# The NSA gate's columns as heads and rests in one stationary of 64 columns, with every queue's order dealt anew

## The chip, the cores and the metric

The kernel runs on one core of one Trainium2 chip. The metric is the device time of one execution in microseconds (us); the kernel before has a median of 608.55 us in three runs.

## The reference, cut to what matters

One layer of a hybrid decoder is computed for a prompt of 512 rows and for 8 sample rows. All 520 rows share one wide input projection, and one small part of it, `a_g`, is the gate of the native sparse attention: 24 columns, three for each of 8 heads.

```
h = x * (1.0 + scale[:, None, :]) + shift[:, None, :]
parts = jnp.split(h @ w_in, np.cumsum(IN_WIDTHS)[:-1], axis=-1)
(a_q, a_kc, a_vc, a_ks, a_vs, a_kw, a_vw, a_g, a_z, b_q, b_k, b_v, b_z, m_a, m_b) = parts
...
o_a = nsa_attention(a_q..., jax.nn.sigmoid(a_g.reshape(bsz, t, NSA_KV, NSA_REP, 3)), ...)
...
return gc[..., 0:1] * o_c + gc[..., 1:2] * o_s + gc[..., 2:3] * o_w
```

The rest: compressed-block, selected-block and sliding-window attention, a second attention over blocks (MoBA), SiLU gates, two up-projections, a merge, an output projection and a layer norm. The sample rows read their keys and values from paged caches in device memory.

## The kernel before

**Products in two parts.** The projection runs on TensorE in fp32r with each fp32 operand split into a head (the value rounded to fp32r) and a rest (value less head). A product is three: head by head, rest of the weights by head of the input, head of the weights by rest of the input. The input, modulated and turned, lies in `hTh` (heads) and `hTl` (rests), 8 blocks of 128 channels by 520 rows. The 520 rows are taken in two halves of 260 (`HB`, `HALF`), one PSUM bank each, so one 128-column part of the projection is 8 blocks x 2 halves x 3 products.

**Weights.** `Feed` loads weights (`load_to`), splits them into heads (ScalarE, L445) and rests (VectorE or GpSimd, L446, by way of L367) in tiles `hl` of two rows of 512 columns (`split_to`), and hands them to `dense` (L688), which issues the products. For the gate `dense("ag", 24)` uses 24 columns for each of the 8 blocks: 192 columns of heads, 192 of rests, 48 products with a stationary of 24 columns. `gen_gates` (L767) reads each half's bank with a Tanh on ScalarE (L771); `gates` (L774) turns the result with five transposes on TensorE, makes the sigmoid of it on VectorE (L779, L781) and hands the samples' values on by small DMAs.

**What runs beside the gate.** The gate belongs to the first list of fills (`FILLS[0]`), which is merged with `phis` (L1130): the compression of cached keys and values, whose pages arrive as `craw` and are split by ScalarE (L1007) and by VectorE or GpSimd (L1008, shown as L367) into tiles `u`, and multiplied into the banks `s`.

**Narrow groups.** Attention's products of probabilities with values (`value`, L1240, bank `o`) have stationaries of 64 columns, and the products for the samples (`dec_a`, `dec_b`, bank `e`) and of the modulation (`ada`, `gen_gate`, bank `s`) of 32 columns; these operands are plain fp32. The dense parts, the scores and the up and output projections are fp32r. One set of products outside the gate has an fp32r stationary below 64 columns: `out_samples` (L1693), 16 columns.

**Order.** `line_up` (L329) fixes the order of each engine's instructions: `QUEUES` holds for each engine a list of places in the order in which the program makes them. `SLOTS` holds which of its buffers each tile takes, in turn; `ps.d` are the three PSUM banks of the dense parts. In both kernels the gate's first half has bank 2 of them and its second half bank 0, and the next dense part takes bank 2 and bank 0 after them. An instruction that waits holds back all that stand behind it on its engine; SP issues nearly all DMAs.

Of the kernel before, what the change touches and what calls it, by code (L numbers as in the profile page):

```python
# [11 lines left out]
AF = mybir.ActivationFunctionType  # L12
# [59 lines left out]
for _name, _w in (("ident", 128), ("seli", 10), ("rowmask", 1), ("ones", 1), ("p16", 1),  # L72
# [24 lines left out]
    "ps.d": "01201201201120112102102102102102102102110120120120120120120122201201201201201221021101201201201201201201201210210210210210210210210210210210"
        "21021",
    "ring.whl": "012012012012012012012012012012012012012012012012012012012012012012012012012012012012012012012012201201201201201",
    "phi.craw": "01230130123012301230",  # L100
# [4 lines left out]
    "at.qx": "0120120120120120",  # L105
    "at.mg": "01010101010101",
    "at.sm": "012345670123456701234567012345670123456701234567012345670123456701234567012345670123456701234567",
    "at.p3": "010101010101010101010101",
    "de.cr": "01201201201201201201201202101201201201201201",
# [19 lines left out]
0-1 5-8 2-3 9-12 20-23 4 13-19 24-49 61-63 50-52 56-57 53-55 58-60 67-69 95-97 64-66 92-94 123-125 70-77 86-88 81-83 89-91 84-85 120-122 78-80 98-105  # L129
109-111 106-108 117-119 148-150 114-116 112-113 126-133 151-153 140-141 179-181 137-139 145-147 142-144 134-136 162-164 154-161 176-178 207-209  # L130
168-169 165-167 170-172 182-189 204-206 222-224 196-197 173-175 201-203 198-200 193-195 190-192 210-218 225-227 231-257 228-230 258-275 219-221
276-281 306-311 324-326 312-317 327-329 351-354 330-332 282-287 333-335 288-293 318-323 336-338 406 339-341 294-299 342-344 358-363 345-350 364-366
300-305 367-372 355-357 373-399 407-412 400-405 413-424 431-435 483-485 425-430 486-488 436-441 489-491 448-453 492-494 442-447 495-497 454-459
498-503 507-509 504-506 460-463 510-515 464-469 516-521 482 531-536 522-527 470-475 528-530 537-542 476-481 555-560 543-554 561-566 579-584 567-572
591-596 585-590 597-602 573-578 672-677 603-608 624-635 648-653 636-638 654-656 639-644 657-659 645-647 609-611 660-671 618-623 696-707 678-689
612-617 720-725 690-695 726-731 708-713 765-767 714-719 768-776 789-794 732-737 795-797 777-779 738-743 780-782 744-749 798-800 783-785 750-755
813-818 786-788 801-809 825-830 810-812 819-824 837-842 849-854 831-836 756-764 855-872 843-848 873-884 906-914 966-971 915-923 885-890 924-926
891-896 927-935 942-947 972-977 936-941 948-959 990-995 897-902 960-965 978-983 903-905 984-989 996-1013 1035-1040 1023-1028 1041-1046 1029-1034
1047-1058 1014-1022 1071-1076 1059-1064 1113-1120 1065-1070 1107-1112 1077-1094 1145 1095-1100 1158 1127-1132 1101-1106 1183-1184 1133-1138 1121-1126
1152-1157 1139-1144 1146-1151 1159-1164 1177-1182 1185-1192 1165-1176 1193-1205 1212 1206-1211 1219-1230 1213-1218 1298-1299 1247-1252 1231-1236  # L140
1243-1246 1237-1242 1253-1258 1284-1285 1260-1265 1272-1277 1259 1266-1271 1278-1283 1306-1307 1314-1319 1300-1305 1320-1321 1328-1329 1286-1297
1336-1337 1344-1345 1322-1327 1330-1335 1308-1313 1352-1355 1338-1343 1346-1351 1362-1367 1382-1387 1380-1381 1376-1379 1374-1375 1356-1361 1368-1373
1388-1405 1412-1417 1406-1411 1418-1433 1458-1463 1436-1437 1434-1435 1468-1473 1444-1447 1474-1475 1448-1449 1456-1457 1438-1443 1450-1455 1464-1467
1476-1483 1506-1517 1504-1505 1494-1495 1484-1493 1522-1523 1502-1503 1524-1529 1496-1501 1534-1547 1566-1571 1530-1533 1558-1563 1518-1521 1576-1579
1548-1551 1564-1565 1580-1585 1572-1575 1552-1557 1586-1599 1602-1607 1600-1601 1628-1635 1616-1627 1658-1659 1612-1615 1660-1665 1674-1681 1642-1645
1636-1641 1608-1611 1652-1657 1646-1651 1668-1673 1666-1667 1682-1687 1690-1695 1700-1705 1688-1689 1726-1731 1734-1739 1742-1747 1708-1713 1706-1707
1718-1725 1766-1769 1696-1699 1748-1753 1740-1741 1756-1761 1754-1755 1714-1717 1778-1783 1792-1795 1732-1733 1770-1777 1806-1809 1784-1791 1816-1817
1762-1765 1800-1805 1810-1815 1796-1799 1829-1834 1844-1849 1827-1828 1854-1859 1824-1826 1835-1840 1842-1843 1850-1853 1841 1818-1823 1860-1863
1900-1903 1924-1927 1882-1884 1872-1875 1885-1887 1864-1865 1890-1895 1866-1871 1876-1881 1896-1899 1910-1915 1904-1909 1930-1935 1888-1889 1928-1929
1952-1957 1918-1923 1984-1989 1960-1965 1916-1917 1970-1973 1998-2001 1940-1943 1958-1959 1974-1979 1936-1939 1982-1983 1944-1951 2016-2017 2002-2009  # L150
1966-1969 2018-2023 2010-2015 2032-2037 2067-2072 1980-1981 2075-2080 1990-1997 2044-2049 2054-2059 2038-2043 2028-2031 2065-2066 2024-2027 2061-2064
2089-2092 2060 2099-2100 2050-2053 2081-2088 2073-2074 2101-2106 2111-2112 2153-2154 2107-2110 2093-2098 2119-2124 2129-2130 2137-2140 2131-2136
2113-2118 2125-2128 2155-2158 2165-2168 2141-2146 2169-2174 2185-2186 2147-2152 2175-2180 2187-2192 2213-2218 2197-2198 2219-2224 2181-2184 2209-2212
2193-2196 2199-2204 2159-2164 2231-2236 2227-2228 2205-2208 2225-2226 2271-2272 2255-2256 2229-2230 2241-2254 2257-2260 2237-2240 2267-2270 2303-2306
2273-2282 2291-2294 2283-2284 2297-2302 2261-2266 2307-2308 2295-2296 2309-2314 2285-2290 2335-2336 2319-2324 2315-2316 2337-2342 2317-2318 2349-2354
2343-2346 2325-2328 2355-2364 2329-2334 2347-2348 2365-2368 2375-2376 2411-2422 2369-2374 2409-2410 2423-2424 2435-2438 2377-2408 2439-2440 2471-2482
2441-2442 2483-2486 2443-2444 2461-2462 2425-2428 2455-2460 2429-2434 2487-2488 2463-2468 2513-2514 2451-2454 2489-2500 2469-2470 2445-2450 2515-2526
2501-2512 2531-2536 2561-2566 2537-2542 2545-2550 2527-2530 2551-2556 2575-2580 2557-2560 2543-2544 2583-2588 2567-2572 2635-2640 2633-2634 2573-2574
2581-2582 2621-2632 2647-2652 2641-2646 2589-2616 2682-2683 2617-2620 2750-2757 2684-2687 2758-2765 2688-2693 2663-2664 2653-2658 2665-2674 2659-2662
2694-2699 2675-2680 2700-2705 2736-2737 2681 2724-2735 2706-2707 2720-2723 2708-2719 2768-2779 2738-2749 2766-2767 2780-2785 2839-2840 2804-2807  # L160
2792-2803 2786-2791 2853-2854 2821-2826 2808-2813 2827-2832 2861-2864 2871-2872 2820 2814-2819 2847-2852 2855-2860 2833-2838 2883-2888 2841-2846
2879-2882 2891 2906-2907 2865-2870 2873-2878 2900-2905 2889-2890 2914-2915 2898-2899 2892-2897 2923-2924 2908-2913 2943-2948 2917-2922 2929-2934
2961-2966 2969-2974 2925-2928 2949-2950 2967-2968 2935-2942 2916 2991-2992 2951-2960 2979-2990 2975-2976 3015-3020 2977-2978 3029-3034 2993-2998
3009-3012 3003-3008 3035-3036 2999-3002 3021-3024 3013-3014 3054-3059 3037-3042 3074-3081 3025-3028 3046-3051 3043-3045 3064-3069 3094-3099 3052-3053
3082-3085 3060-3063 3086-3091 3070-3073 3112-3115 3138-3141 3092-3093 3108-3111 3100-3101 3122-3123 3102-3107 3124-3129 3156-3157 3116-3121 3142-3149
3130-3137 3150-3155 3178-3179 3184-3189 3168-3171 3196-3201 3164-3167 3190-3193 3180-3183 3194-3195 3224-3229 3158-3163 3210-3211 3242-3247 3172-3177
3218-3221 3202-3209 3212-3217 3274-3279 3258-3263 3222-3223 3230-3233 3248-3249 3234-3241 3250-3253 3284-3287 3380-3383 3254-3257 3264-3273 3298-3303
3288-3293 3280-3283 3310-3315 3324-3329 3294-3297 3336-3341 3330-3335 3306-3309 3342-3345 3376-3379 3316-3319 3346-3357 3384-3395 3358-3363 3412-3417
# [175 lines left out]
def build(tc, A):  # L344
# [14 lines left out]
    D = {}  # L359
# [12 lines left out]
    with ExitStack() as es:  # L372
# [35 lines left out]
        class Feed:  # L408
# [23 lines left out]
            def split_to(self, u):  # L432
                while self.ns <= u and self.ns < len(self.units):
# [9 lines left out]
                    if len(src.shape) == 3:  # L443
                        h, l = (t.rearrange("p (a b) -> p a b", a=src.shape[1]) for t in (h, l))
# [1534 lines left out]
```

## Time and profile before

| | us |
|---|---|
| median of three runs (lowest to highest) | 608.55 (608.54 to 608.65) |
| the profiled execution: its time | 609.99 |
| the profiled execution: its span | 608.2 |
| the gate's two Tanh, start | 59.23 and 63.33 |
| PE's last product ends near | 600 |

The profile has one line for each engine's busy time (PE is TensorE's products, PEld its weight loads, DVE VectorE, ACT ScalarE, POOL GpSimd, SP the queue that issues DMAs), a chain of the work that ended last, groups of instructions and waits. Nearly all products are recorded under one helper's line, L351, and the splits into rests under L367, so tiles tell them apart: `d<-hTh,hl 128*24` is a product into bank d from the moving tile hTh and the stationary hl of 128 rows and 24 columns. Products are pipelined: the time of one is its passage, and a busy engine may still have gaps shorter than a passage; the distance between two starts shows the pace. In an entry of waits, the numbers are the total in us, how often, and the longest.

### The profile page before, as it was taken

The page shows a single profiled execution, that of the slowest core. Times are in us where ns is not written, and L with a number is a line of the kernel's source. Part 1 is how long each engine was busy: PE and PEld are TensorE (multiplying, and loading weights), DVE is VectorE, ACT ScalarE, POOL GpSimd, SP SyncE. Part 2 cuts the span into 40 slices and gives each one's busy share as a digit, 9 for nine tenths or more (in the row PEclk, how much of TensorE's full clock was granted, in tenths as well). Part 3 has the DMA queues.
Part 4 walks back from the last instruction along what each step waited for, and adds up shares of the span by engine and source line. Part 5 has one row for each costly group of instructions (what it writes and reads, how often), then busy time and mean ns, then how long its engine had stood idle before and what let it go on. Part 6 is the DMA issues. An engine that isn't in the chain of part 4 may idle for free.

```text
span 608.2 us, 13223 instructions
## 1 busy us (share of the span) xinstructions
PE 590.1 (97%) x4737; PEld 501.8 (82%) x4737; DVE 287.8 (47%) x822; ACT 290.5 (48%) x686; POOL 267.5 (44%) x317
## 2 busy tenths in 40 slices
PE   7999999999999999999999999999999999999994
PEld 4789899999997879778768898997777788889774
DVE  1454455423383567445353435686531144435187
ACT  2457456454555546545435363674632342324343
POOL 0202686372445235434318534546441355554306
PEclk9999999999999999999999999999999999999998
DMA  8987166703555676368888661348899886434403
GB/s 283 405 320 254 43 200 176 247 31 98 151 152 160 190 259 213 121 216 286 273 285 284 246 231 30 113 146 287 301 314 338 312 288 241 144 112 142 172 1 140
DMA packets 63955, 124.79 MB, mean 205 GB/s; under 512 B 8402, under 2 KB 26258, under 8 KB 63378
## 3 DMA queue, kind: packets, MB, share of 16 engines
q1 hardware_dynamic: 62482, 119.76, 58.8%
q0 software_dynamic: 1408, 4.20, 2.1%
q8 instruction: 37, 0.61, 0.4%
q14 instruction: 28, 0.23, 0.1%
HBM read 114.34 MB, written 9.58 MB: 204 GB/s over the span
## 4 chain that ended last, share of the span: by engine, by line
PE 78%; DVE 6%; DMA 5%; ACT 4%; POOL 3%; issue 2%; SPq 1%; POOLq 0%; ACTq 0%; DVEq 0%
PE d L351 45%; PE s L351 13%; PE e L351 7%; PE o L351 6%; PE pt L354 4%; PE pt L351 2%; DMA raw<-mobk 1%; DMA z<-xT 1%; ACT u L1007 1%; SPq L357 1%; DMA raw<-w_cols 1%; DMA raw<-w_up 1%; POOL p L1228 1%; DMA craw<-cmp 1%; DVE hl L367 1%
## 5 line engine op out<-in xcount | busy, mean ns | idle before, releaser
L351 PE MATMUL d<-hTh,hl 128*128 128x260 f32 (+1 forms) x1408 | 267.3, 288 | 1.4 <-ACT ev L771 1.2
L351 PEld LDWEIGHTS d<-hTh,hl 128*128 128x128 f32 (+1 forms) x1408 | 216.2, 187 | 6.5 <-issue 1.4
L351 PE MATMUL d<-hTl,hl 128*128 128x260 f32 (+1 forms) x704 | 198.7, 282 | 0.0
L367 POOL TENSOR_TENSOR hl<-raw,hl 128x512 fp32r<-128x512 f32 x57 | 74.4, 1307 | 139.9 <-ACT hl L445 118.5
L351 PEld LDWEIGHTS d<-hTl,hl 128*128 128x128 f32 (+1 forms) x704 | 131.1, 186 | 0.3
L445 ACT CAST hl<-raw 128x512 fp32r<-128x512 f32 x111 | 67.4, 617 | 81.0 <-PE d L351 46.5
L1226 ACT ACTIVATE p<-s,sm 128x512 f32<-128x512 f32 (+3 forms) x96 | 50.6, 528 | 67.8 <-DVE sm L1223 51.3
L1228 POOL TENSOR_SCALAR p<-p,sm,gp 128x512 f32<-128x512 f32 (+3 forms) x64 | 42.0, 666 | 72.7 <-DVE sm L1227 41.8
L367 DVE TENSOR_TENSOR hl<-raw,hl 128x512 fp32r<-128x512 f32 (+1 forms) x54 | 42.1, 783 | 49.8 <-ACT hl L445 44.5
L351 PE MATMUL d<-yh,hl 128*128 128x260 f32 x256 | 47.4, 285 | 0.0
L351 PEld LDWEIGHTS d<-yh,hl 128*128 128x128 f32 x256 | 40.1, 188 | 3.2 <-ACT yh L851 0.8
L354 PE MATMUL pt<-cst,p 128*128 128x128 f32 x240 | 39.4, 278 | 1.2 <-POOL p L1228 0.8
L1223 DVE CUSTOM_DVE_ANT_0 s<-s,band 128x256 f32<-128x256 f32 (+1 forms) x48 | 17.3, 367 | 41.6 <-PE s L351 33.7
L351 PE MATMUL d<-yl,hl 128*128 128x260 f32 x128 | 36.1, 284 | 0.2 <-DVE yl L367 0.2
L354 PEld LDWEIGHTS pt<-cst,p 128*128 128x128 f32 x240 | 27.4, 141 | 9.5 <-issue 3.1
L351 PE MATMUL s<-kd,q 128*128 128x256 f32 (+3 forms) x96 | 33.5, 351 | 1.5 <-DVE c L1269 0.8
L1236 ACT COPY pp<-pt 128x512 f32<-128x512 f32 (+1 forms) x48 | 22.9, 478 | 24.8 <-PE pt L354 23.8
L351 PE MATMUL s<-u,w1h 128*128 128x256 f32 (+1 forms) x160 | 33.5, 281 | 0.1
L351 PE MATMUL o<-pp,v 128*64 128x512 f32 (+3 forms) x192 | 30.7, 444 | 0.0
L351 PE MATMUL s<-kd,qx 128*128 128x256 f32 (+3 forms) x96 | 30.5, 323 | 0.0
L1228 POOL TENSOR_SCALAR p<-p,sm,cst 128x384 f32<-128x384 f32 (+3 forms) x32 | 21.1, 667 | 16.3 <-DVE sm L1227 16.2
L1221 DVE TENSOR_REDUCE sm<-s 128x1 f32<-128x128 f32 (+1 forms) x48 | 16.5, 352 | 24.3 <-PE s L351 20.6
(411 smaller groups left out, 1037.2 us busy)
## 6 DMA issues: line engine op xcount, KB each, us to landing
raw<-w_cols SPq DMA_DIRECT2D x46, 512.0 KB
raw<-mobk SPq DMA_DIRECT2D x64, 256.0 KB
raw<-mobv SPq DMA_DIRECT2D x64, 256.0 KB
craw<-cmp SPq DMA_DIRECT2D x64, 128.0 KB
u<-ada_ss SPq DMA_DIRECT2D x12, 512.0 KB
raw<-slck SPq DMA_DIRECT2D x64, 64.0 KB
raw<-ada_g SPq DMA_DIRECT2D x8, 512.0 KB
raw<-w_up SPq DMA_DIRECT2D x8, 512.0 KB
```

Source lines behind the costliest of these rows:

```text
L351: return mmraw(out, lhsT, rhs, start=start, stop=stop, skip_group_check=True)
L354: return nc.tensor.transpose(out, x, unit)
L357: return nc.sync.dma_start(out, x)
L367: (nc.gpsimd if eng == "p" else nc.vector).tensor_sub(out, x, f32(hi))
L445: nc.scalar.copy(h, src)
L1007: nc.scalar.copy(dh, src)
L1221: nc.vector.tensor_reduce(sm[:, 0:1], s[:, :b], axis=AX, op=OP.min)
L1223: nc.vector.tensor_tensor_reduce(out=s[:, b:n], in0=s[:, b:n], in1=j.band[:, 256 - (n - b):], scale=1.0, scalar=top, op0=OP.add, op1=OP.mi ...
L1226: nc.scalar.activation(pr, s[:, :n], AF.Exp, scale=-1.0, bias=sm[:, 1:2], accum_out=sm[:, 2:3])
L1228: D.setdefault("pool", []).append(nc.gpsimd.tensor_scalar(pr, pr, sm[:, 3:4], j.gate(i), op0=OP.mult, op1=OP.mult))
L1236: j.copied[gi] = (nc.scalar.copy if COPY_ENG[gi] == "a" else nc.vector.tensor_copy)(t[:, :n], p[:, :n])
```

## The change

The gate's heads and rests are put side by side. For each of the 8 blocks, the weights are padded with zeros from 24 to 32 columns, and the split writes 32 columns of heads and 32 of rests next to each other, so that one stationary of 64 columns holds both. Each block and half then has two products, with `hTh` and with `hTl`: 8 x 2 x 2 = 32 for 48. Rows 0 to 23 of the bank hold heads of the weights by the whole input, rows 32 to 55 rests of the weights by the whole input (with the rest by rest term, which was left out before). ScalarE copies rows 32 to 55 to rows 64 to 87 of the buffer `ev`, VectorE adds rows 0 to 23 of the bank to that, and the Tanh runs on the sum in place. That is two copies and two adds more; the loads, the splits and the rest of the program are the same in number.

```diff
-                    if len(src.shape) == 3:
+                    if n == 256:
+                        h, l = (hl[:, 0].rearrange("p (a x b) -> p a x b", a=8, x=2)[:, :, x] for x in range(2))
+                    elif len(src.shape) == 3:
...
-                return (lambda t: ld(t, A["w_ag"])), 192, [lambda r: r[:, :192]]
+                return (lambda t: ld(t, A["w_ag"])), 256, [lambda r: r[:, :256].rearrange("p (a b) -> p a b", a=8)]
...
         def gen_gates():
-            acc = yield from dense("ag", 24)
-            tg = row("ev", 2)[:24]
+            expect("ag")
+            acc = [p_d(), p_d()]
+            hl = W.use()
             for bk in range(2):
-                D["ev"] = nc.scalar.activation(tg[:, HALF[bk]], acc[bk][:24, :HB], AF.Tanh, scale=0.5)
+                for k in range(8):
+                    for x, hb in enumerate((hTh, hTl)):
+                        mm(acc[bk][:64, :HB], hl[:, 0, k * 64:k * 64 + 64], hb[:, k, HALF[bk]], k == 0 and x == 0, k == 7 and x == 1)
+                    if k % 2 == 1:
+                        if posts and bk and k == 7:
+                            posts.pop(0)()
+                        yield 666
+            ev = row("ev", 2)
+            tg, rest = ev[:24], ev[64:88]
+            for bk in range(2):
+                nc.scalar.copy(rest[:, HALF[bk]], acc[bk][32:56, :HB])
+                nc.vector.tensor_add(tg[:, HALF[bk]], acc[bk][:24, :HB], rest[:, HALF[bk]])
+                D["ev"] = nc.scalar.activation(tg[:, HALF[bk]], tg[:, HALF[bk]], AF.Tanh, scale=0.5)
             post(lambda: gates(tg))
```

All five lists of `QUEUES` and many strings of `SLOTS` are replaced. Of the new lists, the stretches around the gate are shown; three dots stand for what is left out.

```
PE, new:
... 282-285 313-318 335-338 319-321 286-289 322-324 290-297
325-330 342-344 298-301 345-356 302-305 357-359 306-309 360-362 390 363-365 339-341 331-334 366-389 415-419 ...
ACT, old:
... 51 46 28 58 63 69 61 59 64 53 62 57 ...
ACT, new:
... 51 36 62 28 58 63 60 59 65 67
64 61 70-71 52 ...
DVE, new:
... 71 62 84 88 86 76 85 57 78 ...
```

In the new list of PE, 282 to 309 and 331 to 334 are the gate's products, 366 to 389 the 24 wide products after them (12 for each half), 415 to 419 the gate's transposes. In the old list of ACT, 58 and 59 are the gate's Tanh, 69 and 61 casts of cache pages. In the new one, 58 and 60 are the two copies, 59 and 61 the two Tanh, 65 a split of weights, and 63, 67 and 64 casts of pages. In the new list of DVE, 84 and 85 are the two adds, 86 a split, 76 a one-column copy out of bank s.

More of the change, by code (lines that the diff above doesn't have):

```diff
@@ L87 @@
 SLOTS = {
-    "phi.u": "01010101010101",
-    "ring.wr": "0123012031203120312031203120312031203120312031202132013210312033112031320",
+    "phi.u": "01010010101010",
+    "ring.wr": "0133212023011031201301023120203102130321030123331202130231132102313021302",
     "kv.v2": "010101010",
-    "kv.ev": "010101010101010100110011001100110101",
-    "kv.kd": "012021021021021",
+    "kv.ev": "010101010101010011001100110011010101",
+    "kv.kd": "012021021012012",
     "kv.kl": "01",
     "start.xr": "0123",
-    "ps.s": "0101010101010101010101010101010101010101010101010101010101010101010101010101010101010101010101010101010101010101010101010101",
+    "ps.s": "0101010101011010101010110100101101101011010010101001100010110011001101010101100110011001001110101100110101010101010101011001",
     "start.a": "01010101",
[L97 to L100, printed above, removed]
+    "ps.d": "01210201201112002012102010202102120120110210210221012021021002201201200120201210210110210102120120012102102102101202102120220212102120221011"
+        "20210",
+    "ring.whl": "012012021021020120210120120120120120102102101202102012102102101202102101201201201020120120102012012012021210120",
+    "phi.craw": "13200130120321302031",
     "phi.sst": "0",
@@ L133 @@
[L133 to L136, printed above, removed]
@@ L229 @@
[L229 to L231 removed]
+0-1 5-8 2-3 20-23 9-12 24-27 4 13-17 34-35 18-19 36-41 31-33 28-30 42-55 58-63 56-57 67-69 95-97 64-66 92-94 70-77 89-91 81-83 123-125 86-88 84-85
@@ new lines @@
+78-80 120-122 98-105 109-111 151-153 114-116 106-108 148-150 112-113 126-133 117-119 140-141 145-147 176-178 137-139 142-144 134-136 162-164 154-161
+170-172 165-169 179-181 207-209 182-189 204-206 222-224 196-197 193-195 173-175 201-203 198-200 190-192 210-212 225-227 231-233 219-221 213-215
+228-230 216-218 246-251 234-239 252-257 240-245 258-263 270-275 264-269 276-281 310-312 282-285 313-318 335-338 319-321 286-289 322-324 290-297
+325-330 342-344 298-301 345-356 302-305 357-359 306-309 360-362 390 363-365 339-341 331-334 366-389 415-419 403-408 391-396 409-414 397-402 420-425
@@ new lines @@
+444-447 432-437 467-475 426-431 476-481 491-493 482-484 438-443 494-496 515-520 466 497-505 485-490 506-508 454-459 509-511 521-526 448-453 460-465
+527-538 512-514 539-544 551-562 545-550 563-574 587-592 602-616 575-586 632-634 656-673 617-622 635-637 623-628 638-643 629-631 644-655 680-685
+674-679 692-697 686-691 698-703 749-757 704-709 716-721 758-760 710-715 761-763 593-595 764-766 773-775 596-598 776-781 722-733 767-769 782-784
+797-802 770-772 599-601 785-787 734-739 803-808 821-826 788-793 827-832 794-796 833-844 857-862 809-820 863-868 845-856 869-880 890-907 914-916
@@ new lines @@
+908-910 917-922 911-913 740-742 926-931 923-925 950-955 932-934 944-949 935-937 743-748 962-967 938-943 956-961 968-979 1007-1012 986-991 980-985
+1013-1018 992-997 881-889 1019-1042 1055-1060 1043-1048 998-1006 1049-1054 1097-1104 1061-1066 1079-1090 1129 1091-1096 1067-1072 1142 1105-1116
+1167-1170 1073-1078 1117-1128 1136-1141 1183 1130-1135 1143-1154 1161-1166 1171-1176 1155-1160 1177-1182 1196 1184-1195 1203-1208 1215-1220 1197-1202
+1282-1283 1209-1214 1268-1269 1231-1236 1227-1230 1221-1226 1237-1242 1244-1249 1298-1300 1243 1250-1255 1290-1291 1301-1305 1270-1275 1256-1267
@@ new lines @@
+2811-2816 2845-2848 2831-2836 2798-2803 2863-2866 2804 2839-2844 2817-2822 2855-2856 2825-2830 2849-2854 2873-2875 2882-2883 2857-2862 2867-2872
+2876-2881 2884-2889 2892-2897 2907-2908 2901-2906 2913-2918 2927-2934 2945-2950 2953-2958 2909-2912 2951-2952 2898-2899 2919-2926 2961-2962 2935-2938
+2900 2975-2982 2959-2960 2939-2944 2993-2996 2963-2974 2999-3004 2987-2992 3013-3018 2997-2998 3019-3020 2983-2986 3005-3008 3021-3026 3030-3035
+3060-3065 3038-3043 3009-3012 3036-3037 3078-3083 3028-3029 3048-3053 3058-3059 3066-3069 3027 3070-3073 3044-3047 3074-3077 3054-3057 3096-3099
@@ new lines @@
+4173-4178 4188-4202""",
+    "Activation": """
+0 7 3 9 8 1 10-11 5 4 12 6 13-14 2 15-22 24 23 29 25-26 30 38 31 37 39 32 34 27 40 42 33 41 44 43 45 47 46 49 35 50 48 51 36 62 28 58 63 60 59 65 67
+64 61 70-71 52 56 66 69 72 68 57 53-55 84 74 73 80 83 88 85 87 86 91-92 82 81 76 90 77 94 103 89 110 106 93 78 101 97 104 79 111 114 107 102 105 115
+113 112 98 127 117 99 118 121 125 109 95 132 75 133 100 116 96 128 122 129 126 136 131 130 135 137 123 134 147 142 141 140 124 150 144 119 148 143 120
@@ new lines @@
+443-444 452 442 447 454 445 458 446 448 457 460 451 455 453 459 465 461-462 466 464 463 468 467 476 470 456 469 472-473 471 474-475 478 480 477 482
+481 484 483 488-489 485 494 491 495 479 486 501 493 492 497 500 498 490 515 502 496 487 503-504 512 514 505-506 499 511 510 507 513 508-509 518 516
+519 517 523 522 520-521 528 524 533 529 525 534 531 535 532 530 538 536 540-541 539 527 537 543 545 544 549 542 551 546 550 526 547 554 553 555 548
+560 552 556 561 557 559 558 563 562 567 569 568 570 572 571 564-565 575 574 576-577 573 579 578 580-585 566""",
+    "DVE": """
@@ new lines @@
+263 259-260 267 264 268 262 272 261 265-266 258 269 277-278 273 271 274 279 275 284 270 276 280 283 289 285 281 286 282 290 288 295 291 293-294 287
+296 300 292 297 301 299 298 302-303 307 304-306 308-312""",
+    "SP": """
+1 0 7 2 8 3 10 4 34 9 6 5 11-13 15 14 16-19 22 21 20 26 23-25 27-28 33 40 29 38-39 41 58 32 37 42 50 43-47 52 31 35 53-57 36 59-63 51 64-69 71-75 109
+76-80 70 83-87 82 88-97 99-103 98 104-108 110-115 30 116-120 138 122-131 81 133-137 140 132 121 139 141 149-158 142 146 180 159-163 144 164-173
@@ new lines @@
+175-179 181-185 145 187-191 174 241 193-197 208 198-202 148 203-207 235 209-213 192 214-218 238 186 220-234 147 219 242-246 240 236 143 237 239 247
+254 248-252 259-263 253 255-256 48 264-268 286 271-275 269 276-280 257 298 281-285 287-296 270 299-303 305-309 327 258 49 310-314 304 316-320 322-326
+328-332 334-338 333 297 321 315 341 343 347 353 339 345-346 348-352 357 356 363 355 340 367 354 365 358-362 342 368 372-376 370 387 371 369 366
+377-386 388-392 470 344 394-398 404 447 399-403 405-409 445 466 393 434 421 410-414 420 415-419 422-432 435-439 433 440-444 450-454 446 499 467 449
@@ L232 @@
+364 455 474 460 448 468 497 475 469 500 461 471 465 459 479 494 456-457 472 478 458 495 473 476-477 481 480 462 484 496 482 485 483 486 498 487-488
+491 501 490 464 463 492 489 493 502 506-509 504-505 510-512 503 513""",
 }
@@ L1910, in _prepare @@
     d["w_cols"] = f(np.stack([wt[:, :, cols(n)].transpose(1, 0, 2).reshape(128, 1024) for n in COLS]))
-    d["w_ag"] = f(wt[:, :, o["ag"]:o["ag"] + 24].transpose(1, 0, 2).reshape(128, 192))
+    ag = np.zeros((128, 8, 32), np.float32)
+    ag[:, :, :24] = wt[:, :, o["ag"]:o["ag"] + 24].transpose(1, 0, 2)
+    d["w_ag"] = ag.reshape(128, 256)
     w1 = inp["phi_w1"][0].reshape(2, 2, 8, 2, 64, 64)
```

165 lines of the change are left out of this document (67 added, 98 removed).

## The prediction

> **What bounds the kernel now.** I read the page's busy times and chain first, then the same stretches as windows, then what TensorE (PE) itself waited for.
>
> ```profile
> PE 590.1 (97%) x4737; PEld 501.8 (82%) x4737; DVE 287.8 (47%) x822; ACT 290.5 (48%) x686; POOL 267.5 (44%) x317
> PE 78%; DVE 6%; DMA 5%; ACT 4%; POOL 3%; issue 2%; SPq 1%; POOLq 0%; ACTq 0%; DVEq 0%
> ```
> ```profile
> 0.00:20.00 20.00, 15.44 (x98) 9.57 (x98) 5.70 (x18) 6.23 (x11) 0.76 (x6) 1.00 0.88 312
> ...
> 420.00:500.00 80.00, 79.73 (x646) 59.62 (x645) 26.97 (x77) 31.30 (x79) 30.68 (x36) 1.00 0.90 308
> ...
> 580.00:600.00 20.00, 19.86 (x127) 15.41 (x125) 18.70 (x49) 10.32 (x22) 6.00 (x6) 1.00 0.08 30
> 600.00:608.20 8.20, 0.00 (x0) 0.00 (x0) 4.01 (x10) 1.65 (x5) 4.42 (x5) 0.69 0.51 189
> sum 608.20, PE 590.07 PEld 501.77 DVE 287.80 ACT 290.53 POOL 267.53; mean PE 65.56 PEld 55.75 DVE 31.98 ACT 32.28 POOL 29.73
> ```
> ```profile
> PE s L351 <- DMA u<-ada_ss: 1.9, 1, 1.9
> PE d L351 <- ACT ev L771: 1.2, 1, 1.2
> PE e L351 <- POOL zn L643: 1.1, 1, 1.1
> PE s L351 <- DMA cst<-cst: 1.0, 1, 1.0
> ```
>
> In a window's row the columns are PE, PEld, DVE, ACT and POOL busy, the granted clock, the DMA share and GB/s. PE is busy in 590.07 of 608.20 us at clock 1.00. Of the 18.13 idle, 4.56 lie in the first 20 us (20.00 - 15.44) and 8.20 in the tail, so 5.4 us are left for the 580 us between. The kernel is one uninterrupted row of products there: **the time changes by what the row of products changes**, and at most 5.4 us can be won by better waiting. The second entry, 1.2 us, is the largest single wait after the start, and it belongs to the gate that is changed. The last 20 us run beside DVE (18.70 of 20); they begin when the products before them are done, so a microsecond won before moves all of it.
>
> **Fewer products.** 48 become 32.
>
> ```profile
> L351 PE MATMUL d<-hTh,hl 128*24 128x260 f32 x32 | 6.0, 281 | 0.0
> L351 PE MATMUL d<-hTl,hl 128*24 128x260 f32 x16 | 4.5, 281 | 0.0
> ```
> ```profile
> 49.94 0.40 PE L351 MATMUL d<-hTh,hl 128*24 128x260 f32 x2
> 50.18 0.28 PE L351 MATMUL d<-hTl,hl 128*24 128x260 f32 x1
> 50.30 0.40 PE L351 MATMUL d<-hTh,hl 128*24 128x260 f32 x2
> ...
> 61.36 0.40 PE L351 MATMUL d<-hTh,hl 128*128 128x260 f32 x2
> 61.60 0.28 PE L351 MATMUL d<-hTl,hl 128*128 128x260 f32 x1
> 61.72 0.40 PE L351 MATMUL d<-hTh,hl 128*128 128x260 f32 x2
> ```
>
> The mean of 281 ns is a product's passage and overlaps the next; what counts is the distance between starts. Three products with 24 columns take 50.30 - 49.94 = 0.36 us, and three with 128 columns 61.72 - 61.36 = 0.36: 0.12 us each, whatever the stationary's width. No row has 64 columns with this moving operand; it lies between two widths of equal price, so 0.12 us, and 16 fewer are 16 x 0.12 = **-1.9 us**. The bounds: +0 if each product is lengthened by half, which no row supports, to -1.9.
>
> **The order of PE.** The list is dealt anew, so I wrote both lists out as products (the program's order is the same but for the gate's eight chunks of six, now of four) and counted the places where the kind of stationary changes.
>
> ```profile
> 254.32 0.28 PE L351 MATMUL d<-hTl,hl 128*128 128x260 f32 x1
> 254.53 2.78 PE L351 MATMUL e<-raw,zm 128*32 128x512 f32 x24
> 257.24 0.52 PE L351 MATMUL s<-ck,q 128*128 128x64 f32 x3
> ```
> ```profile
> 254.99 0.13 PEld L351 LDWEIGHTS e<-raw,zm 128*32 128x32 f32 x4 [0.30 <-issue]
> ...
> 256.27 0.13 PEld L351 LDWEIGHTS e<-raw,zm 128*32 128x32 f32 x4 [0.30 <-issue]
> ```
> ```profile
> 219.53 0.28 PE L351 MATMUL s<-kd,qx 128*128 128x256 f32 x1
> 219.74 2.37 PE L351 MATMUL o<-pp,v 128*64 128x512 f32 x16
> 221.95 0.60 PE L351 MATMUL o<-pc,cv 128*64 128x256 f32 x4
> 222.38 0.60 PE L351 MATMUL o<-pc,cv2u 128*64 128x256 f32 x4
> 222.91 0.33 PE L351 MATMUL s<-kd,q 128*128 128x128 f32 x1
> ```
>
> Before a fp32 group of 32 columns the last wide product takes 254.53 - 254.32 = 0.21 us instead of 0.12. Inside, four products take 0.43 (three steps from 254.99 to 256.27), six such groups 2.58, but 257.24 - 254.53 is 2.71. The 64-column groups agree: 0.21 going in, and the last four cost 222.91 - 222.38 = 0.53 where those before cost 222.38 - 221.95 = 0.43. So **a change of kind costs about 0.1 us**, on either side. The old list has 143 changes, the new 122: between wide and 32 columns 55 and 53, wide and 64 columns 22 and 15, 32 and 64 columns 21 and 13, the others (plain fp32 of 128 columns) 45 and 41. The first three fall by 17, which is -1.7; for the four others, without a row as clean, I take 0 (bounds 0 and -0.4). **-1.7 us**, with 0 and -2.1 as ends: it is 0 where the reordered product would have waited anyway.
>
> **The gate's evacuation.** Today the bank of one half is freed by the Tanh that reads it.
>
> ```profile
> 63.75 0.51 PE L351 MATMUL d<-hTh,hl 128*128 128x260 f32 x2 [1.16 <-ACT ev L771]
> ```
> ```profile
> 59.23 0.38 ACT L771 ACTIVATE ev<-d 24x260 f32<-24x260 f32 x1 [1.89 <-POOL hl L367]
> 59.52 0.60 ACT L445 CAST hl<-raw 128x512 fp32r<-128x512 f32 x1
> 62.28 1.14 ACT L1007 CAST u<-craw 128x512 fp32r<-128x512 f32 x2 [2.16 <-DMA craw<-cmp]
> 63.33 0.37 ACT L771 ACTIVATE ev<-d 24x260 f32<-24x260 f32 x1
> ```
>
> The second Tanh stood on ACT behind two casts of cache pages that landed late; PE, wanting that bank, stood 1.16 us. In the new lists the bank is freed by a copy on ACT and an add on DVE, with only one cast between the two copies. Their prices: the nearest rows are the same-sized copy and the DVE operation with a PSUM operand of 260 columns.
>
> ```profile
> L721 ACT COPY ev<-d 128x260 f32<-128x260 f32 x3 | 1.1, 377 | 1.1 <-PE d L351 1.0
> ...
> L797 DVE SCALAR_TENSOR_TENSOR z<-z,d 128x260 f32<-128x260 f32 x8 | 3.4, 422 | 2.0 <-ACT z L796 2.0
> ```
>
> Two copies (0.75 us) and two adds (0.84 us) are added; ACT and DVE are at 48% and 47%, and PE is next to run 24 wide products (2.9 us), the first 12 of them (1.44) in the other bank. Copy and add end some 0.38 + 0.42 us after the last gate product, plus its passage of 0.28: 1.1 us, inside the 1.44. So the 1.16 go. But the Tanh is now later: behind the second copy ACT has the first Tanh (0.38), three casts (0.6 each) and only then the second Tanh, about 0.28 + 0.38 + 0.38 + 1.8 + 0.37 = 3.2 us after the last gate product, and PE reaches the five transposes of its result after 24 products, at 2.9 us, not after 42 as today. I charge 0.3 to 0.5 for that: net **-0.7 us** (bounds -1.16, and +2 if a cast waits for pages as long as the 2.16 above). Behind the transposes PE's whole row waits; the first readers of the gates are attention's products much later, which have ample time. If DVE's add waits in its own queue (a split of 0.7 stands two places ahead of it), the slack of 0.3 is used up and up to 0.5 us of the 1.16 stays.
>
> The rest: the split of w_ag handles 256 columns for 192 (a cast of 0.35 us becomes 0.4), its load 128 KB for 96; both lie in the first 60 us under PE. The other lists (SP, POOL, DVE, ACT) issue the same loads and the same work, dealt in another order. At the start x for the first column block and the first weights are asked for in another order; that can move the 4.56 idle us by 1 either way. In the middle every new meeting can remove or make a wait: nothing in the old trace prices them, so 0, with +4 (about as much idle again as the 5.4) and -2 as ends.
>
> **Sum.** -1.9 - 1.7 - 0.7 = -4.3 us, from the execution's own span of 608.2 to 603.9; the median of the runs is 0.35 above that span, so 608.55 - 4.3 = 604.2.
>
> **The rivals.**
> 1. The new dealing gives the boundaries back: the queues no longer meet as well, idle between start and tail rises from 5.4 by the 1.7 + 0.7 that were won, and only the products remain. For it: the other four queues sat idle half the time only because their orders fitted PE's. Against it: half-idle queues have room. 608.55 - 1.9 = 606.6.
> 2. Products with 64 columns count as a narrow kind. The gate's chunks stand in seven separate places of the new list, 14 changes of 0.1: 608.55 - 4.3 + 1.4 = 605.7. For it: the 64-column rows above pay. Against: those are fp32, and narrow stationaries of the gate's own type, 24 columns above and 16 here, run at the pitch of wide ones without such steps.
>
> ```profile
> L351 PE MATMUL e<-hl,msh 128*16 128x512 f32 x16 | 5.0, 393 | 0.0
> ```
> [...]
>
> 3. New waits take about 3 to 5 of the 4.3 us: no change, 607.4 to 609.7. A likely place is 420 to 500, where DMA is at 0.90: if loads rather than PE set the pace there, what PE wins before is given back.
> 4. **Slower**: the transposes of the gates wait for the late Tanh, and that for pages. The longest wait for pages in the trace:
>
> ```profile
> POOL hl L367 <- DMA craw<-cmp: 12.8, 1, 12.8
> ```
> If the chunk ahead of the second Tanh came that late, PE would stand 12.8 less the 2.9 us of cover: 604.2 + 9.9 = 614.1. It decides from a stand of 5.6 us on (4.3 + 1.2). Against: pages of that chunk are asked for before the outputs now, and the chunk after it no longer stands ahead of the Tanh.
>
> **How the numbers follow.** Forecast 604.2 (its own range 602 to 605.5): 0.56. Rival 1, to 607.3: 0.20. Rival 2: 0.04. Rival 3: 0.11. Rival 4 and slower waits of its size: 0.09. About 0.2%, 1.2 us, can be told from no change here. Faster by more: 0.80; within: 0.11; slower: 0.09. The range goes from 601.6 (the forecast with all 2.1 of the changes and 2 us of idle won) up to 607.6, which takes in rival 1.
>
> **What would show it.** Right: 4721 products in PE's busy row (4737 now), 32 of them 128*64 from the gate at a pitch of 0.12, fewer separate groups of 32 and 64 columns, no wait of PE for ACT at the gate, PE busy near 586. Wrong: gate products at 0.2 us at their edges; PE waiting for ACT at the transposes by over 1 us; PE's idle between 20 and 600 us above 8.

## The result, and the profile after

The changed kernel takes 603.87 us (median of 9 runs, 601.18 to 605.58) against 608.65 us (9 runs, 607.76 to 611.75): a ratio of 0.9908, 95% interval 0.9881 to 0.9935. The forecast was 604.2. The number came out; its working did so only in part. What the order won beyond its term, and what two things that were not forecast took back, nearly cancelled.

The page of the changed kernel: the busy row and the row of the granted clock in 40 slices.

```profile
PE 588.1 (97%) x4721; PEld 504.0 (83%) x4721; DVE 293.2 (49%) x824; ACT 291.3 (48%) x688; POOL 271.5 (45%) x317
...
PEclk9998899999999999999999999999999999999998
```

4721 products, 16 fewer than 4737, as written; PE is still the bound. But two slices of the clock row, near 45 to 75 us, show 8 where the row before had 9 everywhere up to the last slice. The windows of the changed kernel show more (PE, PEld, DVE, ACT, POOL busy, granted clock, DMA share, GB/s):

```profile
20.00:580.00 560.00, 557.36 (x4524) 481.56 (x4524) 269.94 (x762) 275.73 (x658) 260.29 (x301) 0.99 0.62 208
300.00:420.00 120.00, 119.60 (x1105) 103.92 (x1107) 68.70 (x205) 66.97 (x173) 65.89 (x77) 1.00 0.58 200
...
57.00:64.00 7.00, 7.00 (x37) 7.00 (x38) 2.34 (x8) 2.31 (x5) 0.32 (x1) 0.53 0.18 52
```

The same windows of the kernel before:

```profile
20.00:580.00 560.00, 554.76 (x4516) 476.79 (x4516) 259.39 (x748) 272.34 (x650) 256.35 (x301) 1.00 0.62 208
...
300.00:420.00 120.00, 118.00 (x1078) 102.38 (x1078) 64.86 (x204) 65.83 (x172) 61.84 (x73) 1.00 0.59 200
...
57.00:64.00 7.00, 5.84 (x52) 5.46 (x52) 1.35 (x5) 2.95 (x8) 3.67 (x5) 1.00 0.34 94
```

Between 20 and 580 us PE's idle time falls from 5.24 us (560 - 554.76) to 2.64; 1.60 of that falls away in 300 to 420 alone (2.00 to 0.40), where the forecast had nothing. And from 57 to 64 us PE is busy all the time, but issues 37 products at a clock of 0.53. The timeline of PE in the changed kernel (start, duration):

```profile
50.08 0.32 PE L351 MATMUL d<-hTh,hl 128*64 128x260 f32 x1
50.24 0.28 PE L351 MATMUL d<-hTl,hl 128*64 128x260 f32 x1
50.36 0.28 PE L351 MATMUL d<-hTh,hl 128*64 128x260 f32 x1
50.48 0.28 PE L351 MATMUL d<-hTl,hl 128*64 128x260 f32 x1
50.59 0.19 PE L351 MATMUL s<-u,w1h 128*128 128x66 f32 x1
...
54.69 0.30 PE L351 MATMUL s<-u,w1h 128*128 128x66 f32 x1 [0.27 <-ACT u L983]
...
56.96 0.46 PE L351 MATMUL d<-hTh,hl 128*64 128x260 f32 x1
57.21 0.42 PE L351 MATMUL d<-hTl,hl 128*64 128x260 f32 x1
57.43 0.42 PE L351 MATMUL d<-hTh,hl 128*64 128x260 f32 x1
...
63.35 0.54 PE L351 MATMUL d<-hTh,hl 128*128 128x260 f32 x2
63.73 0.28 PE L351 MATMUL d<-hTl,hl 128*128 128x260 f32 x1
63.84 0.40 PE L351 MATMUL d<-hTh,hl 128*128 128x260 f32 x2
```

At 50 us the gate's products with 64 columns follow each other at 0.12 us, after a first step of 0.16 behind a small product, and the next kind follows the last of them by 0.11: next to no price for their width. From 56.96 to about 63.5 us nearly every product starts 0.21 to 0.25 us after the one before, and then 0.12 again; the granted clock of that stretch is 0.50: **half clock for 6.5 us, some 3 us lost** (an estimate, 6.5 x (0.22 - 0.12) / 0.22), in a stretch where PE waited no longer than 0.27 us before. No part of the forecast had that.

ACT at the gate, in the changed kernel:

```profile
62.29 0.36 ACT L784 COPY ev<-d 24x260 f32<-24x260 f32 x1 [0.94 <-PE d L351]
62.68 0.42 ACT L786 ACTIVATE ev<-ev 24x260 f32<-24x260 f32 x1
63.01 0.60 ACT L447 CAST hl<-raw 128x512 fp32r<-128x512 f32 x1
63.52 1.13 ACT L1022 CAST u<-craw 128x512 fp32r<-128x512 f32 x2
64.56 0.41 ACT L786 ACTIVATE ev<-ev 24x260 f32<-24x260 f32 x1
```

The second copy stands in front, and the second Tanh ends at 64.97, before the transposes start (65.73). The margin of 0.76 us rests on the half clock, which held PE back: in a later trace of the same kernel at full clock the Tanh ends at 66.20 and the transposes start at 66.28.

```profile
65.79 0.41 ACT L786 ACTIVATE ev<-ev 24x260 f32<-24x260 f32 x1
```

The waits of PE that are left, of which three stand here, hold neither that bank nor those transposes:

```profile
PE s L351 <- DVE cs L653: 2.2, 1, 2.2
PE e L351 <- POOL zn L645: 1.1, 1, 1.1
...
PE pt L354 <- POOL p L1243: 0.6, 3, 0.2
```

### The profile page after: what moved, and what is told of

The parts are those of the page before. It is cut to its first block, busy times and chain, and to the rows that moved or that the text cites. A ratio compares the mean times of both kernels' runs of the same rounds, so it can differ in the third digit from the quotient of the medians.

```text
span 603.8 us, 13227 instructions
## 1 busy us (share of the span) xinstructions
PE 588.1 (97%) x4721; PEld 504.0 (83%) x4721; DVE 293.2 (49%) x824; ACT 291.3 (48%) x688; POOL 271.5 (45%) x317
## 4 chain that ended last, share of the span: by engine, by line
PE 79%; DVE 6%; DMA 5%; ACT 3%; POOL 2%; issue 2%; SPq 2%; POOLq 0%; ACTq 0%; DVEq 0%
PE d L351 47%; PE s L351 12%; PE e L351 7%; PE o L351 5%; PE pt L354 5%; PE pt L351 2%; SPq L357 2%; DMA raw<-w_cols 2%; DMA u<-ada_ss 1%; DMA raw<-ada_g 1%; DVE bn L1762 1%; DMA raw<-mobv 1%; POOL p L1243 1%; DVE xt L1758 1%; POOL u L367 1%
## 5 line engine op out<-in xcount | busy, mean ns | idle before, releaser
L351 PEld LDWEIGHTS d<-hTl,hl 128*128 128x128 f32 (+1 forms) x704 | 132.5, 188 | 0.0
L367 POOL TENSOR_TENSOR hl<-raw,hl 128x512 fp32r<-128x512 f32 x57 | 77.3, 1356 | 113.8 <-ACT hl L447 91.4
L447 ACT CAST hl<-raw 128x512 fp32r<-128x512 f32 (+1 forms) x111 | 68.0, 617 | 51.4 <-PE d L351 43.9
L1241 ACT ACTIVATE p<-s,sm 128x256 f32<-128x256 f32 (+3 forms) x96 | 50.6, 529 | 71.5 <-DVE sm L1238 47.7
L1243 POOL TENSOR_SCALAR p<-p,sm,cst 128x128 f32<-128x128 f32 (+3 forms) x32 | 20.9, 661 | 38.6 <-ACT pp L1251 16.4
L351 PE MATMUL s<-u,w1h 128*128 128x256 f32 (+1 forms) x160 | 35.0, 287 | 0.6 <-POOL u L367 0.3
L351 PEld LDWEIGHTS s<-u,w1h 128*128 128x128 f32 x160 | 28.2, 198 | 1.2 <-POOL u L367 0.5
```

What stands on the lines that cost most here:

```text
L351: return mmraw(out, lhsT, rhs, start=start, stop=stop, skip_group_check=True)
L367: (nc.gpsimd if eng == "p" else nc.vector).tensor_sub(out, x, f32(hi))
L447: nc.scalar.copy(h, src)
L1241: nc.scalar.activation(pr, s[:, :n], AF.Exp, scale=-1.0, bias=sm[:, 1:2], accum_out=sm[:, 2:3])
L1243: D.setdefault("pool", []).append(nc.gpsimd.tensor_scalar(pr, pr, sm[:, 3:4], j.gate(i), op0=OP.mult, op1=OP.mult))
```

## The experiments

Kernels that were measured together ran on one chip, beside the kernel before; ratios are to that. In all, the changed kernel ran 23 times (mean 603.9 us), and the kernel before 75 times beside the experiments (mean 608.4).

**The two halves apart.** The new gate with the old `QUEUES` and `SLOTS`, its products taking the places of the old ones, copies and adds put in:

```diff
 ACT:
-... 51 46 28 58 63 69 61 59 64 53 ...
+... 51 46 28 58-59 65 60 71 63 61 66 53 ...
 DVE:
-... 62 61 86 78-79 84 76-77 80 ...
+... 62 61 88 84 78-79 86 85 76-77 80 ...
```

In the new list of ACT 58 and 60 are the copies, 59 and 61 the two Tanh; in that of DVE 84 and 85 are the adds.

> The new gate (32 products of 64 columns, copy and add ahead of each Tanh) in the old order of all queues; the second copy and add stand ahead of the two casts that held the bank. The sum as predicted: 1.9 us for the products and 1.16 us for PE's wait at the gate's bank go, the transposes stay where they were (42 wide products after the gate), so nothing is paid there: 3.1 us below the kernel before, some 605.5 us. Rival, that the 64 columns count as a kind of their own (0.1 us at each of 16 edges): 607. Rival, that the lower granted clock (0.5 to 0.6 between 57 and 64 us in the changed kernel's trace) comes from having fewer wide products in that stage: a dip of that size here too, and 3 us more, 608.5.

Measured: 608.37 us (12 runs), ratio 1.0013 (0.9992 to 1.0034): nothing gained. The counterpart, the old gate with the new `QUEUES` and `SLOTS` (each chunk of four products is one of six again, copies and adds left out):

> The old gate (48 products of 24 columns, banks freed by the Tanh) in the new order of all queues. If the order is worth the 1.7 us of the changes of kind, and the wait for the second Tanh stays as it was or grows (it stands behind three casts of pages now): 606.9 to 608 us. If the order is worth more, as the changed kernel's least disturbed runs (601.2 to 602.3) less the 1.9 of the products would have it: 604 us. If the order gains nothing by itself: 608.6. If the dip of the clock belongs to the order: granted clock near 0.5 in a stretch between 50 and 65 us.

Measured: 605.76 us (12 runs), ratio 0.9964 (0.9943 to 0.9985): about half of the whole gain. And the changed kernel again, on the same chip:

> The changed kernel once more, for its two groups of times (601.2 to 602.3 and 605.1 to 605.6). If the 3 us between the groups are the half clock of 57 to 64 us, a profile with a time in the lower group shows full clock there, and one in the upper group shows half clock; if the groups come from elsewhere (transfers), the profile of a lower time shows the same dip. Median 604 us.

Measured: 604.22 us (7 runs), ratio 0.9929 (0.9902 to 0.9956). Its profiled run (605.65) has the half clock at the same place; that of a third set of runs, further down, has none. Of all 23 runs of the changed kernel 7 have a mean clock of 0.993 or less; they take 605.9 us in the mean, the 16 others 603.1. The kernel before has such a clock in 4 of 75 runs, the gate alone in 4 of 12, the order alone in 3 of 12. So the half clock explains a group of long runs, but not all: one run took 605.58 at 0.997, and the profiled run of the third set 606.62 at 0.997; that one started late (see the scatter at the start). Nor does a mean clock say where it was lost: the first of the versions for the start has 0.990 in its profiled run, by half clock from 11 to 18 us and none at the gate (1.00 from 57 to 64 us).

The timeline of PE with the gate alone shows where a gain is lost:

```profile
56.26 0.30 PE L351 MATMUL s<-u,w1h 128*128 128x66 f32 x1 [0.78 <-ACT u L983]
...
62.66 0.51 PE L351 MATMUL d<-hTh,hl 128*128 128x260 f32 x2 [0.83 <-DVE ev L785]
```

PE comes sooner to operands that are not ready: it waits 0.78 us for ACT's `u`, and 0.83 for the add that frees the bank, where the first trace of the kernel before had only the 1.16 at the bank. From the gate's first product to the first wide product after it, both traces of the kernel before take 10.97 us and the gate alone 10.43: of the 1.92 us of 16 products 0.54 is left, before the wait at the bank. From the first product into `pt` (near 21 us) to the gate's transposes it takes 45.92 us, the kernel before 46.69 and 45.48: nothing gained against the second trace. This is the shortest of its 12 runs (607.15), so the longer ones may lose more. In the new order the same stretch of the gate, where it runs at full clock, takes 10.88 with 48 products and 9.57 with 32: 1.31 is left.

The trace of the order alone shows the evacuation by the Tanh without copy and add:

```profile
67.70 0.51 PE L351 MATMUL d<-hTh,hl 128*128 128x260 f32 x2 [0.34 <-ACT ev L771]
```

**The half clock.** The last six gate chunks of the changed kernel, once spread among the small products and once behind them, by PE's list alone:

```diff
 changed kernel to spread:
-... 322-324 290-297 325-330 342-344 298-301 345-356 302-305 357-359 306-309 360-362 390 363-365 339-341 331-334 366-389 ...
+... 322-324 290-293 325-330 294-297 342-347 298-301 348-353 302-305 354-359 306-309 360-362 390 331-334 363-365 339-341 366-389 ...
 changed kernel to bunched:
-... 322-324 290-297 325-330 342-344 298-301 345-356 302-305 357-359 306-309 360-362 390 363-365 339-341 331-334 366-389 ...
+... 322-330 342-362 390 363-365 339-341 290-309 331-334 366-389 ...
```

> The changed kernel with its last six gate chunks (four products each) spread evenly among the products of 66 columns of the same stretch; nothing else moves. Theory A, the half clock of 57 to 64 us comes from a stretch in which PE's array computes little (products of 66 columns every 0.11 us, the gate in lumps between them): the stretch is broken up, no run shows a mean clock below 0.994 (5 of 16 runs of the changed kernel do), and the median falls to that of the undisturbed runs, 602. Theory B, the clock drops for a cause outside this stretch: as often as before, median 604. Beside it the 0.3 us that PE waits for ACT at 54.5 us is covered by four of the moved products.

> The opposite of spreading: the last six gate chunks stand together behind the 37 small products of the stretch. Theory A: 4 us without a wide product, the half clock comes in most runs, 3 us each time, median 605 to 606 and clock at 0.991 or less. Theory B: clock as in the changed kernel (5 of 16 runs), median 604; the gate's later end by itself costs under 0.5 us, since the 24 products that follow use the same banks.

Measured: spread 602.85 us (6 runs, 601.68 to 603.22), ratio 0.991 (0.9893 to 0.9927), clocks 0.995 to 0.997 in all; bunched 608.96 us (12 runs), ratio 1.002 (1.0001 to 1.004), clocks 0.985 to 0.992 in all twelve. The window of the spread version, then of the bunched one:

```profile
57.00:64.00 7.00, 7.00 (x62) 6.82 (x62) 3.21 (x11) 4.53 (x10) 2.59 (x3) 1.00 0.15 42
```
```profile
57.00:64.00 7.00, 7.00 (x36) 7.00 (x37) 1.56 (x4) 0.98 (x2) 0.00 (x0) 0.52 0.16 47
```

62 products at full clock against 36 at half, with nothing moved but 24 products. Theory A holds in what it forecast: the drop belongs to this stretch and to how its small products lie. Why the clock falls there was not shown. Two limits: bunching also uncovers the wait for ACT's `u` (1.11 us at 54.66), so the run of small products is not all that differs; and with the changed kernel's list the drop does not come every time: of the five traces that have this list at the gate, two drop and three do not. The bunched version gives back the whole gain of the change, more than expected: its six runs with a mean clock of 0.988 or less take 610.3 us in the mean, the other six 607.6. The profiled one is its shortest (606.12), so no trace shows where the longer ones lose it. In the spread version the wait for `u` was not covered (0.21 us is left of 0.27).

Was the spread version faster than the changed kernel, or lucky? Both again, on one chip:

> The spread version again, beside the changed kernel on the same chip, for the difference between the two. Theory: no run with a mean clock below 0.994, median about 602.9; 1 to 1.5 us below the changed kernel, which is the half clock's 3 us in a third of its runs. Rival, that the six runs without a dip were luck: clocks and median as those of the changed kernel.

> The changed kernel beside the spread version on the same chip: median about 604, a mean clock of 0.993 or less in about a third of the runs.

Measured: spread 604.02 us (6 runs), ratio 0.9921 (0.9897 to 0.9946), one run at 0.993; changed kernel 603.11 us (7 runs), ratio 0.9909 (0.9877 to 0.9941), two at 0.993 or less. The forecast of 1 to 1.5 us fell: the drops came in 1 run of 12 against 7 of 23, too few runs to call them rarer, and the two versions' times can't be told apart. Part of the reason stands among the spread version's waits between 420 and 500 us; the waits of the first trace of the changed kernel, the one with the half clock, have no such entry:

```profile
PE e L351 <- DMA raw<-mobv: 0.9, 1, 0.9
```

PE comes earlier to pages that do not. The changed kernel's third trace, at full clock, has this wait too (0.7 us): part of what a missing half clock wins is given back here.

**The price of a change of kind.** The changed kernel with ten more changes: groups of 32 columns cut five times, at three places. The last of them in PE's list, with three cuts:

```diff
-... 3440-3443 3424-3427 3468-3471 3502-3505 3490-3495 3506-3544 ...
+... 3440-3443 3490-3495 3424-3427 3506-3511 3468-3471 3512-3517 3502-3505 3518-3544 ...
```

> The changed kernel with ten more changes of kind: at four places groups of fp32 products with 32 columns are cut into pieces with six wide products between them. Theory: each change costs 0.1 us, so these stretches are longer by 1.0 us in all, read from the starts of the same products in both traces. Rival: a change costs nothing, and the gain of the order came from waits alone: no longer.

The timeline of PE with the pieces, and of the changed kernel at the same place:

```profile
476.99 0.50 PE L351 MATMUL d<-hTh,hl 128*128 128x260 f32 x2
477.34 0.28 PE L351 MATMUL d<-hTl,hl 128*128 128x260 f32 x1
477.46 0.40 PE L351 MATMUL d<-hTh,hl 128*128 128x260 f32 x2
477.69 0.28 PE L351 MATMUL d<-hTl,hl 128*128 128x260 f32 x1
477.91 1.06 PE L351 MATMUL s<-raw,cs 128*32 128x512 f32 x8
478.90 0.51 PE L351 MATMUL d<-hTh,hl 128*128 128x260 f32 x2
```
```profile
479.94 1.04 PE L351 MATMUL s<-raw,cs 128*32 128x512 f32 x8
480.80 2.21 PE L351 MATMUL e<-raw,tp 128*32 128x512 f32 x16
482.94 0.51 PE L351 MATMUL d<-hTh,hl 128*128 128x260 f32 x2
```

Six wide products between two groups take 477.91 - 476.99 = 0.92 us for 6 x 0.12 = 0.72, and eight of 32 columns between wide ones 0.99 for the 0.86 inside a group. That is 0.20 + 0.13 for two changes, 0.16 each. Read from the starts of the same products, the stretches around the three places are longer by 1.1 us in all, **0.11 a change**, as expected: in the changed kernel they hold some 0.3 us of waiting that is gone with the cuts (the group of 16 above takes 2.14 us for 4 x 0.43; one of its weight loads stood behind pages, 1.01 us of PEld's idle time ended by `raw<-mobv`). The whole run took 603.76.

**The scatter at the start.** Three profiled executions lost 4 us before 20 us: the order alone, the changed kernel's third set and the products put back. The order alone, then the changed kernel's first trace:

```profile
15.25 2.06 PE L351 MATMUL e<-zn 128*128 128x256 f32 x4
17.10 0.87 PE L351 MATMUL s<-cst,a 128*128 128x10 f32 x4
17.81 2.06 PE L351 MATMUL e<-zn 128*128 128x256 f32 x4
19.30 1.00 PE L351 MATMUL d<-hTh,kd 128*128 128x260 f32 x2
```
```profile
12.41 1.11 PE L351 MATMUL e<-zn 128*128 128x256 f32 x4
...
14.10 1.11 PE L351 MATMUL e<-zn 128*128 128x256 f32 x4
14.86 0.59 PE L351 MATMUL d<-hTh,kd 128*128 128x260 f32 x2
```

The same four products take 2.06 or 1.11 us. The changed kernel's third trace, 606.62 us at a mean clock of 0.997:

```profile
15.82 2.01 PE L351 MATMUL e<-zn 128*128 128x256 f32 x4
...
18.79 0.59 PE L351 MATMUL d<-hTh,kd 128*128 128x260 f32 x2
```

Two versions that keep PE busy on zeros, the first from the changed kernel, the second from the spread one:

```diff
-        warm(5)
+        warm(7)
 PE:
-0-1 5-8 2-3 20-23 ...
+0-3 7-10 4-5 22-25 ...
```
```diff
-        warm(5)
+        warm(9)
 PE:
-0-1 5-8 2-3 20-23 9-12 24-27 4 ...
+0-3 9-12 4-5 24-27 6 13-16 7 28-31 8 ...
```

> The changed kernel with two more of the products on zeros that keep PE busy at the start, in the idle time from 3.2 to 5.3 us. Theory: the times of one kernel scatter by some 4 us because PE runs at half clock until 8.5 to 10 us in most runs and until 22 us in some (the profile of the kernel with the order alone shows it: a product on zeros takes 0.43 us there up to 19 us, and 0.21 from 11 us on in the changed kernel), by whether the work of the first microseconds is dense enough. With two more the late rise goes: median 1 to 2 us lower than the changed kernel's 604, scatter between runs halved. Rival: the scatter comes from the transfers, and nothing changes but the chance of a later start.

> The spread version with four more products on zeros at the start: two in the idle time from 3.2 us, and one behind each of the second and third group of the products that wait for transfers (8 to 10.5 us), where the version with only the first two fell back to half clock at 10.7 us until 17.5. Theory: full clock from about 5 us on and no fall; the span is 0.5 to 1 us shorter than the spread version's, median 602, and no run above 603.2. Rival: the transfers set the pace up to 11 us, and the start is no earlier: 602.85.

Measured: 604.79 us (9 runs, 601.85 to 608.01), ratio 0.9943 (0.9919 to 0.9966), and 603.64 us (10 runs, 602.28 to 608.58), ratio 0.993 (0.9905 to 0.9954). Both miss. The timeline of the first shows why more zeros at 3 us do not help:

```profile
5.42 0.64 PE L351 MATMUL s<-u,cs 128*32 128x256 f32 x8 [0.81 <-DVE cs L653]
5.99 1.13 PE L351 MATMUL e<-zn 128*128 128x256 f32 x4
8.11 0.64 PE L351 MATMUL s<-u,cs 128*32 128x256 f32 x8 [0.98 <-DMA u<-ada_ss]
...
11.38 2.08 PE L351 MATMUL e<-zn 128*128 128x256 f32 x4
```

The clock is up at 5.4 us (eight products in 0.64 us) and down again at 11.4 (four on zeros in 2.08 us, for 1.13 at 5.99), after a stretch of short groups that wait for transfers; the first product with `hTh` comes at 17.94 us, 3 late. In the second version's profile the clock was up from 10.3 us on (eight products with `u` in 0.64 us, 1.08 before), but the first product with `hTh` came no earlier (15.83 us against 14.86). What decides which runs start late stays open. Four of eleven traces in the new order do, none of the three in the old.

**The same kernel before, and the products put back.** A second trace of the kernel before, and the spread version with

```diff
+                    mm(acc[bk][:64, HB:512], hl[:, 0, k * 64:k * 64 + 64], hTl[:, k, 0:252], True, True)
```

after each pair of gate products; these change the gates' values, and the outputs that use them.

> The kernel before once more, for a second trace of it: its profiled execution took 609.99 us, 1.4 above the median. Expected 608; if its row of products from 23 us on is shorter than in the first trace (last product ends 576.9 us after that point), the differences between the traces of the two kernels are to be taken against both; PE at full clock between 50 and 65 us.

> The spread version with 16 products put back: after each pair of gate products one of 252 columns with the same stationary goes into the unused part of the bank and is read by nobody. Theory: 16 x 0.12 = 1.9 us more than the spread version's 602.85, 604.8. Rival, that in this stretch PE meets waits that take in the difference (as in the old order, where the 16 products fewer moved the median by less than it can tell): 603.

Measured: the products put back, 605.51 us (10 runs), ratio 0.9945 (0.9927 to 0.9963). Against the spread version's 0.991 and 0.9921 that is 1.5 to 2.1 us more, the lower of them within the noise. But the profiled execution does not bear it out. Its stretch of the gate is longer by 1.26 us (10.79 for 9.53), yet from the first product into `pt` to the last product it takes no longer than the spread version: its idle time between 20 and 580 us is 2.01 against 3.42, and the wait of 0.9 above is gone. The execution took 606.47 because its first product with `hTh` came at 19.80 us for 14.76. So whether the 16 products or late starts lengthen the median is open.

This distance, from the start of the first `pt<-hTh,kd` to that of the last group, `d<-m,v`, leaves the scatter at the start out; the same 104 products stand ahead of it in every version of the table:

| kernel | us, one number for each trace |
|---|---|
| before | 578.49, 577.46 |
| gate alone | 576.01 |
| order alone | 573.03 |
| changed, with the half clock | 574.28, 574.03 |
| changed, without it | 571.69 |
| spread | 571.49, 571.38 |
| spread, products put back | 571.23 |

The order alone is 4.4 to 5.5 us shorter than the kernel before, more than its 2.3 at the median, which holds late starts and drops of the clock too; the half clock costs 2.3 to 2.6. These are single executions, and those of the kernel before took 609.99 and 609.39 us, above their mean of 608.4.

The kernel before took 609.39, and in its second trace the gate's bank makes no wait:

```profile
61.04 1.14 ACT L1007 CAST u<-craw 128x512 fp32r<-128x512 f32 x2 [0.51 <-DMA craw<-cmp]
62.09 0.38 ACT L771 ACTIVATE ev<-d 24x260 f32<-24x260 f32 x1
```

The pages landed 1.24 us earlier (casts at 61.04 for 62.28), so the second Tanh did too. Its idle time between 20 and 580 us is 4.22 us (PE busy 555.78 of 560), against 5.24 in the first.

## Why the prediction came out, point by point

- **Fewer products, -1.9.** Pitch and count are as forecast, and in the new order the stretch of the gate is 1.3 us shorter. How much of that reaches the end is open: 1.5 to 2.1 by the medians with the products put back, nothing by that version's trace. Read as a property of the gate it was wrong: in the old order the same 16 products bring nothing at the median, and the trace shows PE waiting for `u` (0.78 us) and the bank (0.83) instead. Rival 1's mechanism, a gain given back at the next meeting, is real; it was named for the new dealing and is shown for the old.
- **The order, -1.7 by 17 changes of kind.** The price holds where changes were added, 0.11 us each net and 0.16 without waits. The order alone gains 2.3 us at the median and 4.4 to 5.5 behind the start, in which the fewer changes and the waits below are both; how much is which wasn't taken apart. The term was too small for what the order does to the row of products.
- **The gate's evacuation, -0.7.** This was a 1.16 us wait of one execution; the second trace of the kernel before has none. With the new order and the old Tanh 0.34 is left, with copy and add none. The 0.3 to 0.5 charged for late transposes did not come, by a margin of 0.08 us at full clock. The term should have been taken as anything from 0 to -1.2.
- **New meetings in the middle, 0.** Here the size failed. Beyond the gate's 1.16, idle time between 20 and 580 us fell by 1.4 us against the first trace; against the second, 1.6 in all. It lies in 300 to 420 (2.00 and 1.76 us idle before, 0.38 to 0.45 in three traces after) and comes with the order (0.53 with the order alone), though the gate alone in the old order has 0.89. The bounds of -2 and +4 held it, the value taken did not.
- **The half clock.** Not foreseen: 3 us where the profile shows it, and by the mean clock in 7 of 23 runs, so nearly 1 us in the mean. The forecast took the granted clock of 1.00 as given, although the change takes wide products away from the very stretch that holds the small ones.
- **Late starts.** Not foreseen in this size: the forecast gave the start 1 us either way, and three traces in the new order lose 4.
- **The sum.** The half clock and the late starts took back much of what the order had won beyond its term, and so -4.3 met a measured -4.8, and -4.4 between the means of all runs (603.9 and 608.4). How many of the untraced runs start late is not on record, so this share is argued, not shown. That the number is so close is in part luck. Two slips in the working change nothing: 4.3 + 1.2 is 5.5, not 5.6, and the lower end of the range follows from its terms as 601.8, not 601.6.
- **Rival 2, 64 columns as a narrow kind.** Refuted: 0.12 inside, 0.11 to the next kind, and some 0.04 for the first step, not 0.1 on both sides. The fp32 groups of 32 columns do pay at a change of kind (0.11 us each); the gate's type with 64 does not.
- **Rival 4, late Tanh.** Did not come: the Tanh ended at 64.97, the transposes began at 65.73; at full clock it was 66.20 and 66.28.
- **PE busy near 586** was 588.1; without the half clock's 3 us it would have been 585, and the spread version's traces have 584.3 and 585.3.

## What to carry to other kernels

Here one engine bounds, and removing work from it did not pay where the operands behind it came no earlier (16 products fewer in the old order: a ratio of 1.0013, waits of 0.78 and 0.83 us): measure the cut in both orders before giving it a value. A wait seen in one trace is one draw (1.16 us in the first trace of the kernel before, none in the second); take a second trace of the same kernel before putting it into a sum. And in a row of products without a gap, keep the small ones mixed with wide ones: bunching 24 products in one place (a ratio of 1.002, for 0.991 with them spread) cost this kernel all that the change had won. When runs of one kernel scatter by 5 us, compare traces from a product behind the start as well as by their whole time.

## What was not expected of the hardware

The granted clock fell in a row of products that hardly stops: to half for 6.5 us (0.50 from 56.96 to 63.5), with no wait over 0.27 us before it from 20 us on in the changed kernel's trace. The granted clock of this trace, 0.83 in the mean from 50 to 70 us, makes 20 x 0.17 / 0.5 = 6.8 us at half, an estimate that agrees. PE was hardly idle before the drop (busy 6.69 of 6.96 us from 50 to 56.96), only filled for the most part with products of 66 columns, 34 of 59. These start every 0.11 us, hardly closer than one of 260 columns at 0.12. That the clock goes by how many columns pass in a time is argued, not shown. At the start the clock rose between about 8 and 11 us in most profiles (four products on zeros take 2.08 us before and 1.11 to 1.13 after), and near 18 to 22 us in three, 4 us later by the first products with `hTh` (18.79 to 19.80 us, for 14.86); the windows' clock column reads 1.00 there, and only the pitch of the products shows it. In a fourth it rose near 5 and fell again from 11 to 18, where that column shows it (0.83 in the mean from 0 to 20 us).
